# Dilated attention: queries transposed by head and residue, token order copied by GpSimd, and inverse roots by Ln and Exp with one Newton step

## The chip, the cores and the metric

One Trainium2 chip; the kernel runs on one of its cores. The core has engines that work side by side, each through its own queue in order: TensorE (PE in the profile, with its weight loads as PEld), VectorE (DVE), ScalarE (ACT), GpSimd (POOL) and SyncE (SP), which here issues most of the DMA transfers. The metric is the device time in microseconds.

## The reference

One decoder layer over 2048 tokens of width 1024, with 8 attention heads of 64:

```python
h = rms_norm(x, g_mix)
u, gb, gc, q, k, v = split(h @ w_in)
y_conv = gb * short_conv(gc * u, conv_w)
q = rms_norm(q per head, g_q) * HEAD_DIM ** -0.5
k = rms_norm(k per head, g_k)
y_attn = dilated_mixture(q, k, v)
x = x + concat(rms_norm(y_conv), rms_norm(y_attn)) @ w_out
x = x + (silu(h2 @ w_gate) * (h2 @ w_up)) @ w_down      # h2 = rms_norm(x, g_ffn)
```

`rms_norm` is y / sqrt(mean(y^2) + 1e-6) times a gain. `dilated_mixture` evaluates each head three times, with (window, dilation) of (128, 1), (512, 4) and (2048, 16): a query at token t attends to tokens t, t - d, t - 2d, ... within the window. The three outputs of a head are combined with weights in proportion to their softmax denominators. Everything is float32; the kernel gets there with pairs of float16 numbers, a high part and the rest.

## The kernel before, in words

By the trace, the input norm and the convolution's projections take the first 245 us, the first group of q, k and v runs to 300, attention from there to 800, the output projection to 960, the feed-forward network to the end.

Attention works on four head pairs, g = 0 to 3 (`attn_steps`). While pair g is attended, the q, k and v of pair g + 1 are made (`qkv_steps`); beside the last pair runs the rest of the convolution. `attention` draws the two streams together: after each attention step it takes `rate` steps of the other stream, and holds these with `issue_after` behind a mark some `lag` steps back in the attention stream. Within that, the framework's scheduler decides each engine's order (`schedule_with_timeline_sim=True`). Rate and lag are numbers per pair and stay as they are.

`qkv_steps` works in chunks of 512 tokens, 4 for each pair, 16 in all. The 128 rows of a chunk's matmul j are the tokens 4t + j, so a chunk is laid out by residue modulo 4. In a chunk:

- PE makes q, k and v in 4 groups of matmuls into PSUM (L187 to L189); ACT reads q and k out, once as they are (L468) and once squared (L469), and v (L472); DVE takes v's remainder (L473).
- DVE sums the squares (L479) and makes 16 inverse roots for each partition: L480 adds the epsilon, the helper `rsqrt` takes a first guess by integer arithmetic (L45, L46) and does three Newton steps (L48, L49, L50 each), and L482 scales by 2 to the 11th.
- POOL multiplies q and k by the roots (L483) and k by its gain (L486); ACT and POOL split them into high and low parts in `qkhl` (L492 to L495).
- SP issues three DMA transposes (L195): q into `qp`, and the two key tiles `ka` and `kl` (the trace shows `kl` as kb).
- DVE copies `qp` into `qT`, one copy for each head, and in doing so brings the residues back to token order (L504).

`attn_steps` runs, for each head of the pair, the branches b in the order 1, 2, 0, that is dilation 4, 16 and 1. A step is two or four blocks of 128 queries: PE makes scores with the query as the stationary operand and the keys as the moving one (L606, L607, high and low key part), DVE masks them and finds the minimum (L612), ACT takes Exp (L617). Then the weights have to be transposed: most steps do it by ACT's cast (L627), DVE's remainder (L628) and a DMA transpose from `eh` to `et` (L195), the others on PE (L622, L623, L624). PE multiplies with v (L635) and ACT reads the result out (L638). At a head's end `combine` (L542 to L556) joins the three branches, on POOL for every head but the last; DVE makes its weights and ACT their Exp (L546).

In branch 0 the query is a contiguous slice of `qT`, in branch 1 a slice with a stride of 4 elements, in branch 2 one with a stride of 16. The keys lie by residue: contiguous in branch 1, with a stride of 4 in branch 2.

Of the kernel before, what the change touches and what calls it, by code (L numbers as in the profile page):

```python
# [2 lines left out]

# [5 lines left out]
F32 = mybir.dt.float32  # L9
F16 = mybir.dt.float16  # L10
I32 = mybir.dt.int32
AF = mybir.ActivationFunctionType
# [17 lines left out]
class Builder:  # L30
# [167 lines left out]
    def run(self):  # L198
        tc, nc, A = self.tc, self.nc, self.A
        with ExitStack() as ctx:  # L200
# [20 lines left out]
            with ExitStack() as c1:  # L221
                e = c1.enter_context
                self.psmm = e(tc.tile_pool(name="psmm", bufs=3, space=PSUM))
                self.qk = e(tc.tile_pool(name="qk", bufs=4))
# [45 lines left out]
    def conv_steps(self, j, W, before=None, scratch=None):  # L270
# [12 lines left out]
        for c in range(S // NC):  # L283
# [17 lines left out]
            w1 = own[:, 0:2] if own is not None else self.qk.tile([P, 2, NC], F32, name="qT")  # L301
# [26 lines left out]
            nc.scalar.activation(s2, y, AF.Square)  # L328
# [36 lines left out]
    def in_and_conv(self):  # L365
        tc, nc, A = self.tc, self.nc, self.A
        w_in, w_out = A["w_in"][0], A["w_out"][0]
        with ExitStack() as c:
# [23 lines left out]
            def norm(i, n):  # L392
                tags = 6 * ("nx_x",) + ("qT", "qT") + 8 * ("nx_x",)
                self.norm(i, [(self.qk if tg != "nx_x" else xp).tile([P, D], F32, name=tg) for tg in tags[i:i + n]],
# [48 lines left out]
    def qkv_steps(self, g, st):  # L443
# [8 lines left out]
        qT = [self.qk.tile([P, S], F16, name="qT") for _ in range(2)]  # L452

        ka, kl = (self.qk.tile([P, 4, 2, 512], F16, name=nm, bufs=2) for nm in ("ka", "kb"))
        dv = self.d_v[g]
        for i in range(0, NT, 4):
# [22 lines left out]
            nc.vector.tensor_reduce(ss, n, axis=AX.X, op=ALU.add)  # L479
            nc.vector.tensor_scalar(ss, ss, 1.0 / HD, EPS, op0=ALU.mult, op1=ALU.add)  # L480
            r = self.rsqrt(self.at, ss, 16, "qkr")
            nc.vector.tensor_scalar_mul(r, r, 2.0 ** 11)  # L482
# [15 lines left out]
            qp = self.at.tile([P, 2, 4, P], F16, name="qp", bufs=2)  # L498
            for n_, dst in enumerate((qp, ka[:, i // 4].rearrange("p h (j t) -> p h j t", j=4),
                                      kl[:, i // 4].rearrange("p h (j t) -> p h j t", j=4))):  # L500
                self.transpose(dst.rearrange("p h j t -> p (h j) t"),
                               hl[:, 2 * n_:2 * n_ + 2].rearrange("p h j x d -> p (h j x d)"))
            for h in range(2):
                nc.vector.tensor_copy(qT[h][:, i * P:(i + 4) * P].rearrange("p (t j) -> p t j", j=4),  # L504
                                      qp[:, h].rearrange("p j t -> p t j"))
# [3 lines left out]
    def attn_steps(self, g, st):  # L509
# [18 lines left out]
        for h, b in [(h, b) for h in range(2) for b in (1, 2, 0)]:  # L528
            qT = st["qT"][h]
            ka, kl = (st[x][:, :, h] for x in ("ka", "kl"))  # L530
            load_v(h, b)
# [31 lines left out]
            def query(u):  # L563

                if b == 0:
                    return qT[:, u * P:(u + 1) * P]
                if b == 1:
                    return qT[:, u // 4 * 512 + u % 4:(u // 4 + 1) * 512:4]
                return qT[:, u::16]
# [651 lines left out]
```

## Time and profile before

| | |
|---|---|
| runs | 2189.73, 2185.88, 2181.43 us |
| median | 2185.88 us |
| the profiled execution's own time (the span of its trace) | 2189.4 us |
| PE busy over the span | 2068.8 us (94%) |
| DVE | 1457.8 us (67%) |
| ACT | 1025.1 us (47%) |
| POOL | 625.8 us (29%) |
| mean granted PE clock | 0.984 |

The profiled execution has no other time than its span; it lies 3.5 us above the median of the runs. Shares over the whole span hide the stages: half of it is the feed-forward network, in which PE hardly ever waits. The rows to read are those of the stretches from 245 to 800 us. A row of waits names the engine and line that waited, the engine, tile and line that ended the wait, and then the total in us, how often, and the longest one. A row of groups gives the operation with its output and input and its count, then busy us and mean ns of one, then idle time just ahead on the same engine with what ended it.

### The profile page before, as it was taken

The page shows a single profiled execution, that of the slowest core. Times are in us where ns is not written, and L with a number is a line of the kernel's source. Part 1 is how long each engine was busy: PE and PEld are TensorE (multiplying, and loading weights), DVE is VectorE, ACT ScalarE, POOL GpSimd, SP SyncE. Part 2 cuts the span into 40 slices and gives each one's busy share as a digit, 9 for nine tenths or more (in the row PEclk, how much of TensorE's full clock was granted, in tenths as well). Part 3 has the DMA queues.
Part 4 walks back from the last instruction along what each step waited for, and adds up shares of the span by engine and source line. Part 5 has one row for each costly group of instructions (what it writes and reads, how often), then busy time and mean ns, then how long its engine had stood idle before and what let it go on. Part 6 is the DMA issues. An engine that isn't in the chain of part 4 may idle for free. (4 is left out here: it accounts for less than half of the span.)

```text
span 2189.4 us, 32832 instructions
## 1 busy us (share of the span) xinstructions
PE 2068.8 (94%) x11864; PEld 1077.2 (49%) x11864; DVE 1457.8 (67%) x3380; ACT 1025.1 (47%) x2134; POOL 625.8 (29%) x515
## 2 busy tenths in 40 slices
PE   4899999989899889999999999999999999999999
PEld 2344567767666544443444444444444444444444
DVE  5687446778776687795767676756676666545554
ACT  6443346776766656563433333333333334444341
POOL 0000133343443212120232111211121145555463
PEclk9999999999999989999999999999999999999999
DMA  9767458899989996799332233223322663251342
GB/s 245 169 201 243 115 119 153 186 178 178 183 168 202 208 214 216 242 276 263 124 109 87 97 106 101 89 95 101 106 87 97 235 241 105 77 180 54 119 142 96
DMA packets 555492, 339.64 MB, mean 155 GB/s; under 512 B 354624, under 2 KB 508224, under 8 KB 552896
## 3 DMA queue, kind: packets, MB, share of 16 engines
q1 hardware_dynamic: 537648, 314.38, 55.9%
q10 hardware_dynamic: 17680, 23.16, 3.0%
q8 instruction: 93, 1.52, 0.3%
q14 instruction: 71, 0.58, 0.1%
HBM read 161.24 MB, written 107.54 MB: 123 GB/s over the span
## 5 line engine op out<-in xcount | busy, mean ns | idle before, releaser
L1001 PEld LDWEIGHTS <-w 128*128 128x128 f16 x3696 | 362.3, 98 | 454.9 <-issue 20.2
L1001 PE MATMUL ps<-b,w 128*128 128x512 f16 x2112 | 466.5, 382 | 14.0 <-DVE s L1007 6.1
L1132 PE MATMUL ps<-b,w 128*128 128x512 f16 x1848 | 399.8, 379 | 4.0 <-DVE s L1153 2.2
L1001 PE MATMUL ps<-hb,w 128*128 128x512 f16 x1584 | 347.1, 379 | 0.0
L1132 PEld LDWEIGHTS <-w 128*128 128x128 f16 x1848 | 180.8, 98 | 222.9 <-issue 5.4
L187 PE MATMUL mm<-wq,b 128*128 128x384 f16 x512 | 171.8, 335 | 7.1 <-DVE vs L473 7.1
L894 POOL TENSOR_TENSOR t<-wq 128x512 f32<-128x512 f32 (+1 forms) x46 | 59.5, 1294 | 411.4 <-issue 239.0
L1007 DVE TENSOR_TENSOR s<-ps,s 128x512 f32<-128x512 f32 x220 | 150.0, 683 | 34.4 <-PE ps L1001 33.9
L189 PE MATMUL mm<-wq,b 128*128 128x384 f16 x512 | 171.7, 335 | 0.0
L188 PE MATMUL mm<-wq,b 128*128 128x384 f16 x512 | 171.5, 335 | 0.0
L1139 POOL TENSOR_TENSOR x<-x,s 128x512 f32<-128x512 f32 x72 | 103.4, 1436 | 172.6 <-DVE s L1153 134.2
L1140 DVE SCALAR_TENSOR_TENSOR x<-ps,a_u,x 128x512 f32<-128x512 f32 x96 | 71.8, 749 | 100.9 <-PE ps L1132 74.3
L617 ACT ACTIVATE s<-s,u 128x256 f32<-128x256 f32 (+1 forms) x224 | 97.9, 452 | 69.4 <-DVE u L612 50.2
L612 DVE CUSTOM_DVE_ANT_0 s<-s,mask,nkap 128x256 f32<-128x256 f32 (+1 forms) x224 | 104.6, 483 | 19.5 <-PE s L607 13.9
L188 PEld LDWEIGHTS <-b 128*128 128x128 f16 x768 | 84.5, 110 | 67.1 <-issue 18.2
L187 PEld LDWEIGHTS <-b 128*128 128x128 f16 x768 | 84.4, 110 | 61.5 <-ACT b L775 6.4
L911 ACT CAST w<-t 128x512 f16<-128x512 f32 x88 | 53.7, 616 | 127.4 <-PE ps L1001 61.9
L189 PEld LDWEIGHTS <-b 128*128 128x128 f16 x768 | 84.2, 110 | 57.2 <-issue 5.2
L187 PE MATMUL cvx<-b,wq 128*128 128x512 f16 (+1 forms) x200 | 77.0, 388 | 32.1 <-ACT kb L264 24.8
L635 PE MATMUL av<-v,et 128*128 128x65 f16 x1800 | 77.7, 195 | 28.1 <-DMA et<-eh 18.7
L606 PE MATMUL s<-ka,qT 128*128 128x128 f16 (+1 forms) x408 | 91.8, 272 | 10.3 <-DVE eh L628 9.2
L1120 DVE TENSOR_TENSOR w<-t,w 128x512 f16<-128x512 f32 (+1 forms) x96 | 75.3, 801 | 34.2 <-ACT w L1119 33.9
(297 smaller groups left out, 3773.4 us busy)
## 6 DMA issues: line engine op xcount, KB each, us to landing
d_a<-a ACTq DMA_DIRECT2D x88, 256.0 KB, 2.0
d_wd<-w SPq DMA_DIRECT2D x77, 256.0 KB, 2.1
wq<-d_a SPq DMA_DIRECT2D x64, 256.0 KB, 4.2
b<-d_wd SPq DMA_DIRECT2D x14, 1024.0 KB, 6.3
wraw<-in_w_in_dram SPq DMA_DIRECT2D x24, 512.0 KB, 7.2
d_h<-hl SPq DMA_DIRECT2D x24, 512.0 KB, 3.2
wq<-in_w_gate_dram SPq DMA_DIRECT2D x22, 512.0 KB, 5.3
wq<-in_w_up_dram SPq DMA_DIRECT2D x22, 512.0 KB, 5.2
```

The source lines that it names most:

```text
L187: self.pe = mm(ps, lhsT=lh(k), rhs=rh(k), start=k == ks[0], stop=False)
L188: mm(ps, lhsT=lh(k), rhs=rl(k), start=False, stop=False)
L189: mm(ps, lhsT=ll(k), rhs=rh(k), start=False, stop=k == ks[-1])
L606: nc.tensor.matmul(o, lhsT=query(u), rhs=hi[x], start=True, stop=False)
L612: nc.vector.tensor_tensor_reduce(sm[:, at[u]], sp[:, at[u]], mask[:, P - P * has_prev(u):256], accum_out=Ub[:, u, HD + 1:HD + 2], op0=ALU.add,
L617: nc.scalar.activation(sm[:, at[u]], sm[:, at[u]], AF.Exp, scale=-1.0, bias=Ub[:, u, HD + 1:HD + 2])
L635: self.pe_av = nc.tensor.matmul(av[:, u - u0], lhsT=p_, rhs=v_, start=n_ == 0, stop=n_ == len(ops) - 1)
L1001: nc.tensor.matmul(ps[self.BANK[n]], lhsT=w[:, x, k], rhs=b[:, y, k], start=first and k == 0 and q == 0, stop=k == 3 and q == 2, skip_grou ...
L1007: nc.vector.tensor_tensor(t, x, y, op=ALU.add)
L1120: nc.vector.tensor_tensor(L[n][:, 1, 0:n_f], src[n], L[n][:, 0, 0:n_f], op=ALU.subtract)
L1132: nc.tensor.matmul(ps[self.BANK[n]], lhsT=L[n][:, x, f], rhs=B[n][:, f, y], start=first and f == 0 and q == 0, stop=f == n_f - 1 and q == ...
L1139: nc.gpsimd.tensor_tensor(o, o, s_, op=ALU.add)
```

## The change

*The query.* `qT` becomes one tile for both heads, laid out as head, residue j, chunk n, position t. The DMA transpose writes straight into it, so `qp` and DVE's 32 copies are gone. At the start of each head (b == 1) GpSimd copies that head's queries into token order, into a tile `qn` with one buffer, in 4 copies of 128x512. Branch 0 reads `qn`, contiguous as before. Branch 1 now reads a contiguous slice of `qT`, branch 2 one with a stride of 4.

*The inverse roots.* ACT takes Ln of the mean square plus epsilon and Exp of minus half of that plus 11 ln 2, which is the root already scaled by 2 to the 11th; DVE does one Newton step on it. A table that holds both functions is loaded behind the last Square of the convolution, where before the table for Exp was loaded ahead of the first L617; the number of table loads is the same, 5.

*Buffers.* The pool `qk` loses two of its four default buffers, and what shared the tag `qT` (a tile of the convolution, tiles of the norm and of the output projection) takes tiles of twice the size from it.

```diff
--- before.py
+++ after.py
@@ -1,5 +1,6 @@
 from contextlib import ExitStack, nullcontext
 from itertools import chain, islice
+import math
 
 import concourse.bass as bass
 import concourse.tile as tile
@@ -221,7 +222,7 @@
             with ExitStack() as c1:
                 e = c1.enter_context
                 self.psmm = e(tc.tile_pool(name="psmm", bufs=3, space=PSUM))
-                self.qk = e(tc.tile_pool(name="qk", bufs=4))
+                self.qk = e(tc.tile_pool(name="qk", bufs=2))
                 self.mixer(c1)
 
                 self.fs = ctx.enter_context(tc.tile_pool(name="fs", bufs=1, side="right"))
@@ -298,7 +299,7 @@
                 return ps, u
             gc, u = yield from gemm(2)
             own = scratch if c == 0 else None
-            w1 = own[:, 0:2] if own is not None else self.qk.tile([P, 2, NC], F32, name="qT")
+            w1 = own[:, 0:2] if own is not None else pair(c, "qT").rearrange("p (a b) -> p a b", a=2)
             gcs, a = w1[:, 0], w1[:, 1]
             nc.scalar.activation(gcs, gc, AF.Copy, scale=u)
             yield True
@@ -325,7 +326,7 @@
             acc = self.sq[:, c] if j < 3 else s2
             if j == 0:
                 s2 = acc
-            nc.scalar.activation(s2, y, AF.Square)
+            self.sqr = nc.scalar.activation(s2, y, AF.Square)
             if 0 < j < 3:
                 nc.gpsimd.tensor_tensor(acc, acc, s2, op=ALU.add)
                 s2 = acc
@@ -390,8 +391,8 @@
                 W[m] = self.weights([cols(0)[m]], ux, dst=(t0[:, 0, :, cs], t0[:, 1, :, cs]), raw=raw0[:, m])
 
             def norm(i, n):
-                tags = 6 * ("nx_x",) + ("qT", "qT") + 8 * ("nx_x",)
-                self.norm(i, [(self.qk if tg != "nx_x" else xp).tile([P, D], F32, name=tg) for tg in tags[i:i + n]],
+                two = self.qk.tile([P, 2, D], F32, name="qT") if i <= 6 < i + n else None
+                self.norm(i, [two[:, k - 6] if k in (6, 7) else xp.tile([P, D], F32, name="nx_x") for k in range(i, i + n)],
                           [t[:, j] for tg in ("ka", "kb")[i % 4 // 2:(i % 4 + n) // 2]
                            for t in (self.qk.tile([P, 2, 2, D], F16, name=tg, bufs=2),) for j in range(2)])
             spills = []
@@ -449,8 +450,7 @@
         u = self.uq[:, g:g + 1]
         st["u"] = u
         yield
-        qT = [self.qk.tile([P, S], F16, name="qT") for _ in range(2)]
-
+        qT = self.qk.tile([P, 2, 4, 4, P], F16, name="qT")
         ka, kl = (self.qk.tile([P, 4, 2, 512], F16, name=nm, bufs=2) for nm in ("ka", "kb"))
         dv = self.d_v[g]
         for i in range(0, NT, 4):
@@ -477,9 +477,14 @@
             ff = f.rearrange("p a b d -> p (a b) d")
             ss = self.at.tile([P, 16], F32, name="qk_ss")
             nc.vector.tensor_reduce(ss, n, axis=AX.X, op=ALU.add)
+            r = self.at.tile([P, 16], F32, name="qkr_y")
+            t = self.at.tile([P, 16], F32, name="qkr_t")
+            nc.scalar.activation(t, ss, AF.Ln, scale=1.0 / HD, bias=self.lnb[:, 0:1])
+            nc.scalar.activation(r, t, AF.Exp, scale=-0.5, bias=self.lnb[:, 1:2])
             nc.vector.tensor_scalar(ss, ss, 1.0 / HD, EPS, op0=ALU.mult, op1=ALU.add)
-            r = self.rsqrt(self.at, ss, 16, "qkr")
-            nc.vector.tensor_scalar_mul(r, r, 2.0 ** 11)
+            nc.vector.scalar_tensor_tensor(t, r, -0.5 * 2.0 ** -22, r, op0=ALU.mult, op1=ALU.mult)
+            nc.vector.tensor_tensor(t, t, ss, op=ALU.mult)
+            nc.vector.scalar_tensor_tensor(r, t, 1.5, r, op0=ALU.add, op1=ALU.mult)
             nc.gpsimd.tensor_tensor(n, ff, r.unsqueeze(2).broadcast_to([P, 16, HD]), op=ALU.mult)
             n4 = n.rearrange("p (a b) d -> p a b d", a=4)
             nk = n4[:, :, 2:4]
@@ -495,14 +500,10 @@
                 nc.gpsimd.tensor_tensor(hl[:, 4 + h, :, 0], k, hl[:, 2 + h, :, 0], op=ALU.subtract)
 
 
-            qp = self.at.tile([P, 2, 4, P], F16, name="qp", bufs=2)
-            for n_, dst in enumerate((qp, ka[:, i // 4].rearrange("p h (j t) -> p h j t", j=4),
-                                      kl[:, i // 4].rearrange("p h (j t) -> p h j t", j=4))):
-                self.transpose(dst.rearrange("p h j t -> p (h j) t"),
-                               hl[:, 2 * n_:2 * n_ + 2].rearrange("p h j x d -> p (h j x d)"))
-            for h in range(2):
-                nc.vector.tensor_copy(qT[h][:, i * P:(i + 4) * P].rearrange("p (t j) -> p t j", j=4),
-                                      qp[:, h].rearrange("p j t -> p t j"))
+            for n_, dst in enumerate((qT.rearrange("p h j n t -> p (h j) n t")[:, :, i // 4],
+                                      ka[:, i // 4].rearrange("p h (j t) -> p (h j) t", j=4),
+                                      kl[:, i // 4].rearrange("p h (j t) -> p (h j) t", j=4))):
+                self.transpose(dst, hl[:, 2 * n_:2 * n_ + 2].rearrange("p h j x d -> p (h j x d)"))
             yield
         st.update(qT=qT, ka=ka, kl=kl)
 
@@ -526,8 +527,13 @@
                 for r in range(4):
                     nc.sync.dma_start(t[32 * r:32 * r + 32], dv.rearrange("(n p r) c -> r p n c", n=NT, r=4)[r])
         for h, b in [(h, b) for h in range(2) for b in (1, 2, 0)]:
-            qT = st["qT"][h]
+            qT = st["qT"][:, h]
             ka, kl = (st[x][:, :, h] for x in ("ka", "kl"))
+            if b == 1:
+                qn = self.at.tile([P, S], F16, name="qn", bufs=1)
+                for n in range(4):
+                    nc.gpsimd.tensor_copy(qn[:, n * 512:(n + 1) * 512].rearrange("p (t j) -> p t j", j=4),
+                                          qT[:, :, n].rearrange("p j t -> p t j"))
             load_v(h, b)
 
 
@@ -563,10 +569,10 @@
             def query(u):
 
                 if b == 0:
-                    return qT[:, u * P:(u + 1) * P]
+                    return qn[:, u * P:(u + 1) * P]
                 if b == 1:
-                    return qT[:, u // 4 * 512 + u % 4:(u // 4 + 1) * 512:4]
-                return qT[:, u::16]
+                    return qT[:, u % 4, u // 4]
+                return qT[:, u % 4].rearrange("p n t -> p (n t)")[:, u // 4::4]
 
             def keys(tl, u, prev):
 
@@ -695,6 +701,11 @@
         nc.vector.tensor_scalar_mul(self.kap, u, HD ** -0.5 * 2.0 ** -22)
         nc.vector.tensor_scalar_mul(self.nkap, self.kap, -1.0)
 
+        with self.tc.issue_after(self.sqr.ins):
+            nc.scalar.preload_act_table_set("natural_log_exp_and_others")
+        self.lnb = self.at.tile([P, 2], F32, name="lnb")
+        nc.vector.memset(self.lnb[:, 0:1], EPS)
+        nc.vector.memset(self.lnb[:, 1:2], 11 * math.log(2.0))
         self.qkhl = self.at.tile([P, 6, 4, 2, HD], F16, name="qkhl")
         nc.gpsimd.memset(self.qkhl[:, 4:6, :, 1], 0.0)
         self.y7 = self.rows.tile([P, NT, HD], F32, name="y7")
@@ -768,7 +779,7 @@
             ya = tk[:, 0].rearrange("p a (b c) -> p (a b) c", c=2 * P).rearrange("p k (j t) -> p k j t", j=2)
         else:
             ya = self.op.tile([P, 4, 2, P], F32, name="ya")
-        xk = self.qk.tile([P, 2, D], F32, name="kb", bufs=2) if p % 3 == 1 else None
+        xk = self.qk.tile([P, 2, D], F32, name="kb" if p % 3 == 1 else "qT")
         for j in range(2):
             nc.sync.dma_start(ya[:, :, j], self.d_ya[:, :, (p + 8 * j) * P:(p + 8 * j + 1) * P])
         for k in range(4):
@@ -778,7 +789,7 @@
         self.x1[p] = []
         for j in range(2):
             i = p + 8 * j
-            x1 = self.qk.tile([P, D], F32, name="qT") if xk is None else xk[:, j]
+            x1 = xk[:, j]
             nc.sync.dma_start(x1, self.A["x"][0][i * P:(i + 1) * P])
             t = tk[:, 1, j] if p < 2 else self.op.tile([P, 512], F32, name="xt", bufs=2)
```

Line numbers after the change are up by 1 until L480 or so, and by 6 in the attention steps: L612 becomes L618, L617 L623, L627 L633, L628 L634, L638 L644; POOL's L483, L486, L494, L495 become L488, L491, L499, L500, and its L550 to L556 become L556 to L562.

First, DVE around one chunk's inverse roots, during pair 0's attention. ISA is the mask with the minimum (s is a tile of scores), qk_ss the sums of squares, qkr_i, qkr_y and qkr_t the root's tiles. Before:

```order
L480 TENSOR_SCALAR qk_ss<-qk_ss 128x16
L612 ISA s,u<-s,mask,nkap 128x256
L612 ISA u 128x1
L45 TENSOR_SCALAR qkr_i<-qk_ss 128x16
L612 ISA s,u<-s,mask,nkap 128x256
L612 ISA u 128x1
L46 TENSOR_SCALAR qkr_y<-qkr_i 128x16
L48 SCALAR_TENSOR_TENSOR qkr_t<-qkr_y 128x16
L49 TENSOR_TENSOR qkr_t<-qkr_t,qk_ss 128x16
L628 TENSOR_TENSOR eh<-s,eh 128x512
L50 SCALAR_TENSOR_TENSOR qkr_y<-qkr_t,qkr_y 128x16
L553 RECIPROCAL bm<-u 128x16
```

And after the change:

```order
L479 TENSOR_REDUCE qk_ss<-qkn 128x16
L473 SCALAR_TENSOR_TENSOR vs_2120<-mm,vs_2120 128x2x64
L634 TENSOR_TENSOR eh<-s,eh 128x512
L618 ISA s,u<-s,mask,nkap 128x256
L618 ISA u 128x1
L484 TENSOR_SCALAR qk_ss<-qk_ss 128x16
L634 TENSOR_TENSOR eh<-s,eh 128x512
L485 SCALAR_TENSOR_TENSOR qkr_t<-qkr_y 128x16
L618 ISA s,u<-s,mask,nkap 128x256
L618 ISA u 128x1
L486 TENSOR_TENSOR qkr_t<-qkr_t,qk_ss 128x16
L487 SCALAR_TENSOR_TENSOR qkr_y<-qkr_t,qkr_y 128x16
```

Before, the rows shown end in the first Newton step, and seven more rows of the root come behind them (two more steps of L48 to L50, the last rows between masks again, and L482), twelve behind L480 in all. After, three rows behind L484 (which is L480) end the root. The two copies of q for each chunk (L504) have no rows any more.

Second, ACT at the same chunk, after the change (before it there is nothing of the root on ACT):

```order
L633 CAST eh<-s 128x512
L623 ACTIVATE s<-s,u 128x256 x2
L482 ACTIVATE qkr_t<-qk_ss,lnb 128x16
L633 CAST eh<-s 128x512
L483 ACTIVATE qkr_y<-qkr_t,lnb 128x16
L644 COPY u<-av 128x4x65
L623 ACTIVATE s<-s,u 128x256
L468 ACTIVATE qkf<-mm,uq 128x256
```

Ln (L482) stands between the Exp and the cast of score tiles, and Exp of the root (L483) behind that cast. Ln needs DVE's L479, and DVE's L485 needs this Exp.

Third, POOL between a chunk of pair 1 and the combine of a head of pair 0. Before:

```order
L495 TENSOR_TENSOR qkhl<-qkn,qkhl 128x4x64 x2
L550 TENSOR_TENSOR r_3072<-r_3072,cw 128x16x65
L550 TENSOR_TENSOR r_3336<-r_3336,cw 128x16x65
L551 TENSOR_TENSOR r_3072<-r_3072,r_3336 128x16x65
L550 TENSOR_TENSOR u<-u,cw 128x16x65
L552 TENSOR_TENSOR u<-u,r_3072 128x16x65
L556 TENSOR_TENSOR u<-u,bm 128x16x64
L483 TENSOR_TENSOR qkn<-qkf,qkr_y 128x1024
```

And after:

```order
L500 TENSOR_TENSOR qkhl<-qkn,qkhl 128x4x64 x2
L535 COPY qn<-qT 128x512 x4
L556 TENSOR_TENSOR r_3028<-r_3028,cw 128x16x65
L556 TENSOR_TENSOR r_3281<-r_3281,cw 128x16x65
L557 TENSOR_TENSOR r_3028<-r_3028,r_3281 128x16x65
L556 TENSOR_TENSOR u<-u,cw 128x16x65
L488 TENSOR_TENSOR qkn<-qkf,qkr_y 128x1024
L558 TENSOR_TENSOR u<-u,r_3028 128x16x65
```

The four copies into token order stand between the last remainder of a chunk (L500) and the combine (L556), and the next chunk's multiplication by the roots (L488) has moved ahead, into the middle of the combine.

## Prediction

> **What bounds the kernel now.** I read the windows first, one stretch for each stage, since an edit inside attention can only be priced in the stretches where attention runs. The columns are the stretch, its length, then busy time and instruction count of each engine, the granted clock, the share of the DMA engines and their rate:
>
> ```profile
> core 0: us, PE busy (x) PEld busy (x) DVE busy (x) ACT busy (x) POOL busy (x), PEclk, DMA share, GB/s
> 300.00:660.00 360.00, 327.26 (x3167) 250.82 (x3165) 264.83 (x959) 245.99 (x664) 133.07 (x105) 0.96 0.91 175
> 660.00:800.00 140.00, 123.79 (x1149) 79.44 (x1148) 100.68 (x385) 84.12 (x214) 32.24 (x21) 0.94 1.01 219
> 960.00:1790.00 830.00, 815.97 (x3757) 368.09 (x3756) 565.21 (x1032) 319.32 (x567) 180.82 (x145) 0.99 0.42 129
> ```
>
> PE carries the kernel, and the stretch that this change touches is 300 to 660, where three head pairs run with the next pair's q, k and v between them. PE is idle there for 360.0 − 327.3 = 32.7 us. DVE is the busiest of the others (264.8 of 360, 74%), ACT has 68%, POOL 37%, and the DMA engines 0.91. In 660 to 800 the last pair runs without any q and k work. The feed-forward stretch behind it belongs to PE and isn't touched. So no more than 32.7 us of waits, plus whatever PE's own work gets shorter, can be won.
>
> Then PE's waits in that stretch (total us, times, longest):
>
> ```profile
> PE s L606 <- DVE eh L628: 8.9, 6, 2.6
> PE av L635 <- DMA et<-eh: 7.2, 10, 2.0
> PE mm L187 <- DVE vs L473: 6.9, 5, 2.2
> PE av L635 <- DMA v<-d_v: 4.6, 1, 4.6
> PE av L635 <- ACT u L638: 1.8, 1, 1.8
> PE av L635 <- ACT qkn L469: 1.3, 1, 1.3
> PE s L606 <- DVE u L612: 1.1, 2, 0.9
> PE pt L622 <- ACT sm L617: 0.5, 1, 0.5
> PE av L635 <- DVE et L624: 0.3, 1, 0.3
> ```
>
> These add up to 32.6 us, all of PE's idle time. DVE ends 8.9 + 6.9 + 1.1 + 0.3 = 17.2 us of it: PE waits for a PSUM tile that DVE hasn't read out. The et transposes on the DMA queue end 7.2 us, ACT 3.6 us.
>
> **What DVE loses.** The groups of 245 to 800 on DVE (count, then busy us and mean ns, then idle time just ahead and its releaser):
>
> ```profile
> L504 DVE COPY qT<-qp 128x512 f16<-128x512 f16 x32 | 29.9, 976 | 19.3 <-DMA qp<-qkhl 19.2
> L479 DVE TENSOR_REDUCE qk_ss<-qkn 128x16 f32<-128x1024 f32 x16 | 19.5, 1218 | 12.3 <-ACT qkn L469 12.2
> L50 DVE SCALAR_TENSOR_TENSOR qkr_y<-qkr_t,qkr_y 128x16 f32<-128x16 f32 x48 | 10.6, 222 | 1.1
> L48 DVE SCALAR_TENSOR_TENSOR qkr_t<-qkr_y 128x16 f32<-128x16 f32 x48 | 9.4, 197 | 1.0
> L49 DVE TENSOR_TENSOR qkr_t<-qkr_t,qk_ss 128x16 f32<-128x16 f32 x48 | 8.3, 172 | 1.0
> L45 DVE TENSOR_SCALAR qkr_i<-qk_ss 128x16 int32<-128x16 int32 x16 | 5.8, 362 | 0.1
> L482 DVE TENSOR_SCALAR qkr_y<-qkr_y 128x16 f32<-128x16 f32 x16 | 4.7, 297 | 0.4
> L46 DVE TENSOR_SCALAR qkr_y<-qkr_i 128x16 int32<-128x16 int32 x16 | 4.7, 297 | 0.8
> ```
>
> All 32 copies of L504 go (29.9 us), the seed and the final scaling (L45, L46, L482: 15.2 us), and two of three Newton steps (two thirds of 10.6 + 9.4 + 8.3, 18.9 us). That is 64.0 us of DVE time, and with it the 19.2 us in which DVE, an in-order queue, stood still ahead of L504 until the transpose of q had landed. The DMA issues of 300 to 800 (count, median us to landing) show how much of it lies there:
>
> ```profile
> et<-eh SPq DMA_TRANSPOSE x112, 4.2
> qp<-qkhl SPq DMA_TRANSPOSE x14, 3.3
> ```
>
> 14 of the 16 chunks come after 300, so about 56 us leave 300 to 660: DVE falls from 264.8 to about 209 of 360, 58%.
>
> What PE gets of it can't be read off directly. Both large DVE-ended waits are queueing: L628 and L473 are short, but stand behind other DVE work. A queue's wait goes roughly with busy over idle share: 0.74/0.26 = 2.8 now, 0.58/0.42 = 1.4 then, a half less; the blocking ahead of L504 goes too. I estimate that 65% of the 17.2 us goes: **−11.2 us** (bounds: 0, if other engines are late at the same places, and 17.2). The second late thing is the et transpose, which starts when L628 on DVE has written eh. SP waits for that:
>
> ```profile
> SPq L195 <- DVE eh L628: 45.3, 23, 6.4
> SPq L195 <- POOL qkhl L495: 9.9, 4, 4.4
> ```
>
> If L628 comes earlier, the transposes are issued earlier, but they keep their own 4.2 us. I take a third of the 7.2 us: **−2.4 us** (0 to 7.2).
>
> **The query's stride on PE.** Branch 1 read its query with a stride of 4 elements and now reads it contiguously; branch 2 goes from a stride of 16 to 4. The keys, the moving operand, stay as they are, with a stride of 4 in branch 2. First two score matmuls of branch 1, then some of branch 2 with the weight loads beside them (start, duration):
>
> ```profile
> 285.33 0.22 PE L606 MATMUL s<-ka,qT 128*128 128x128 f16 x1
> 285.38 0.22 PE L607 MATMUL s<-kb,qT 128*128 128x128 f16 x1
> ...
> 342.49 0.28 PE L606 MATMUL s<-ka,qT 128*128 128x128 f16 x1
> 342.60 0.30 PE L607 MATMUL s<-kb,qT 128*128 128x128 f16 x1
> 342.71 0.30 PE L606 MATMUL s<-ka,qT 128*128 128x128 f16 x1
> ...
> 342.33 0.14 PEld L606 LDWEIGHTS <-qT 128*128 128x128 f16 x1
> 342.50 0.14 PEld L607 LDWEIGHTS <-qT 128*128 128x128 f16 x1
> ...
> 456.36 0.30 PE L607 MATMUL s<-kb,qT 128*128 128x128 f16 x1
> 456.48 0.34 PE L187 MATMUL mm<-wq,b 128*128 128x384 f16 x1
> ```
>
> Branch 1 starts a matmul every 0.05 to 0.06 us, branch 2 every 0.12. So stride 4 in the weights costs nothing, and branch 1 gains nothing. In branch 2 both operands are strided. The matmul at 342.49 had its weights loaded from 342.33 to 342.47, under the matmul before it, and the next one still starts 0.11 us later; and the last branch-2 matmul, at 456.36, holds up a matmul with another weight tile for 0.12 us. Both point to the moving keys, which the change leaves alone. Branch 2 has 2 × 16 score matmuls in each of 8 heads, 256. If the weights set the pace, 256 × 0.064 = 16.4 us would go; if the keys do, almost nothing. By those two rows I take **−2 us**.
>
> [...]
>
> **What is added to ACT.** 16 chunks × 2 activations of 128x16. The nearest row is a small Exp:
>
> ```profile
> L546 ACT ACTIVATE cw<-cw 128x48 f32<-128x48 f32 (+1 forms) x11 | 2.7, 241 | 8.5 <-DVE cw L545 8.4
> ```
>
> 32 × 0.241 = 7.7 us of ACT, 14/16 of it in the stretch: 246 goes to 253, 70%. The table load only moves. Each chunk now also crosses from DVE to ACT (Ln needs L479's sum) and back (the Newton step needs Exp's result). ACT works in order, so a Ln whose sum is late holds the Exp of scores (L617) behind it, and with it the mask and cast for PE. I raise ACT's 3.6 us by a half: **+1.8 us** (0 to 28, the third rival).
>
> **What is added to POOL and SP.** 32 copies of 128x512 f16. The bounds are a memset of that size and a two-operand f32 operation of that size:
>
> ```profile
> L699 POOL MEMSET qkhl<- 128x512 f16 x1 | 0.5, 524 | 0.0
> L486 POOL TENSOR_TENSOR qkn<-qkn,gk 128x512 f32<-128x512 f32 x16 | 20.4, 1278 | 1.2
> L483 POOL TENSOR_TENSOR qkn<-qkf,qkr_y 128x1024 f32<-128x1024 f32 x16 | 30.5, 1903 | 177.1 <-DVE qkr_y L482 175.3 <-ACT s L617 1.7
> ```
>
> The copy reads with a stride, so I take the upper end, 1.25 us: 40 us in all (17 to 41), some 30 of them in 300 to 660, where POOL goes from 133 to about 163 of 360. They hide in POOL's idle time (177 us ahead of L483 alone), and their result isn't wanted until the third branch. What isn't hidden: four in a row (5 us) ahead of a combine and of the next chunk's L483, whose end (L495) SP's transposes wait for. SP's in-order queue has the et transposes behind them. 5 us more on SP's 9.9, a third of it reaching PE: **+1.7 us** (0 to 10). The transposes move the same bytes. If POOL's cover were gone, all 40 us would stand in the q and k chain.
>
> **Sum.** −11.2 − 2.4 − 2.0 + 1.8 + 1.7 = −12.1 us. The profiled span, 2189.4, lies 3.5 above the median of 2185.88; the saving is taken from either, so 2177.3 for a like profile, and **2174 us** for the median.
>
> **The rivals.** About 11 us (0.5%) is what a measurement of this kernel can tell from no change.
>
> *Another wait takes over: 2183 us.* L628 itself waits: the view of 300 to 660 has it idle behind ACT's cast,
>
> ```profile
> L628 DVE TENSOR_TENSOR eh<-s,eh 128x512 f16<-128x512 f32 (+1 forms) x80 | 54.0, 677 | 20.7 <-ACT eh L627 20.4
> ```
>
> and the DMA share is 0.91 to 1.01. Then ACT or the transposes are late where DVE was, and only about half of the 6.9 us for L473 goes, −3 us. Against it: DVE is the busiest engine beside PE.
>
> *The weights set branch 2's pace: 2160 us.* −12.1 − (16.4 − 2.0) = −26.5. For it: the weight load at a stride of 16 lasts 0.14 us, and the only slow branch is the only one with it. Against: the rows at 342.49 and 456.36.
>
> *ACT's queue is stalled by the crossings: 2198 us.* Place: Ln at the head of ACT's queue, twice 16 crossings. Price: ACT's present waits for DVE,
>
> ```profile
> ACT s L617 <- DVE u L612: 40.3, 27, 5.7
> ```
>
> are 1.5 us each. 32 × 1.5 + 7.7 = 56 us of ACT; with half of it reaching PE, +28 against −15.6 of gains, +12. It decides from about 0.9 us a crossing on. For it: L479 lasts 1.2 us and stands behind other work on DVE. Against: the instructions ahead in ACT's queue are often late themselves, and DVE has become shorter.
>
> **Chances.** The forecast gets 0.46: its terms are sized by rows, except for the 65%. Its own range, 2165 to 2183, has the bound of 2175 inside it, and I put 0.32 of the 0.46 below that bound and 0.14 above. Another wait gets 0.24, the weights 0.14, ACT's queue 0.16. Faster: 0.32 + 0.14 = 0.46; same: 0.14 + 0.24 = 0.38; slower: 0.16. Since cases of both signs are in it, the range that should hold 8 in 10 goes from 2152, below the weights' 2160 by the 6 us that DVE's term could still gain, plus 2 for et, to 2200, just past ACT's case.
>
> **What would show it.** DVE's busy time in 300 to 660 near 209 us, and L606's and L473's waits on DVE at a third; the et waits on DMA near 5 us. Branch 2's matmuls still 0.12 us apart: keys; 0.06: weights. POOL's copies near 1.25 us. ACT's Ln with an idle time ahead of it well under 0.9 us each. I'm wrong if PE's idle time in that stretch stays near 33 us, or if ACT's idle time ahead of Ln goes beyond 30 us.

## The result and the profile after

The changed kernel takes 2169.53 us (median of 4 runs, 2166.6 to 2174.52) against 2186.85 us before (4 runs, three of which stood ahead of the prediction): a ratio of 0.9926, 95% interval 0.9908 to 0.9944, or 17.3 us less. The forecast was 2174, with 2152 to 2200 as its range. The two profiles lie further apart than the medians, 2189.4 and 2165.8 us, or 23.6, since the profiled execution of before was the slowest of its four and that of after lies below its median; so the differences between the two profiles below are some 6 us too large in all.

The windows were cut at the first score matmul and the last product with v, which lie at 285.3 and 803.5 us before and at 285.0 and 776.4 after. Windows of the profile before (columns as above: stretch, length, busy time of PE, PEld, DVE, ACT, POOL, PE clock, DMA share, GB/s):

```profile
285.30:803.50 518.20, 469.25 (x4436) 342.48 (x4434) 375.14 (x1377) 338.20 (x897) 171.96 (x131) 0.96 0.91 182
803.50:2189.00 1385.50, 1357.16 (x6247) 612.13 (x6245) 896.32 (x1556) 564.75 (x1000) 427.77 (x339) 0.99 0.45 138
```

The same two stretches of the profile after:

```profile
285.00:776.40 491.40, 457.83 (x4441) 335.17 (x4440) 330.50 (x1212) 340.96 (x921) 202.49 (x162) 0.98 0.95 192
776.40:2165.00 1388.60, 1360.48 (x6243) 612.79 (x6239) 899.17 (x1564) 565.16 (x1000) 427.86 (x339) 0.99 0.45 138
```

All of the gain lies in attention: 518.2 − 491.4 = 26.8 us; behind it 3.5 us are lost (2189.4 − 803.5 against 2165.8 − 776.4). In attention PE's idle time falls from 48.9 to 33.6 us (−15.4), and its busy time by 11.4 us for the same matmuls, at a granted clock of 0.98 in place of 0.96. Over the whole span the clock differs by 0.002 only (0.984 and 0.986). DVE loses 45 us, POOL gains 31.

PE's waits in attention, after the change (total us, times, longest):

```profile
PE av L641 <- DMA et<-eh: 22.1, 20, 4.2
PE av L641 <- ACT u L644: 6.5, 5, 2.3
PE s L612 <- DVE eh L634: 2.3, 2, 1.7
PE mm L188 <- ACT b L786: 1.2, 1, 1.2
PE av L641 <- DVE et L630: 1.1, 1, 1.1
```

And those of before that answer to them, over its attention:

```profile
PE av L635 <- DMA et<-eh: 18.7, 19, 3.0
PE s L606 <- DVE eh L628: 9.2, 7, 2.6
...
PE av L635 <- DVE et L624: 1.5, 4, 0.6
```

With L473's 6.9 and L612's 1.1, DVE ended 18.7 us of PE's waits before and 3.4 us now, 15.3 less. The one wait for v (4.6 us) is gone too. The waits for et grew by 3.4 us, and those for ACT's read-out of av (L644) by 4.7.

The work of the new root and of the copies, groups of 245 to 777 after the change. On DVE the first two of four rows are shown (L486 and L487 are 4.6 and 2.7 us more), then ACT and POOL:

```profile
L484 DVE TENSOR_SCALAR qk_ss<-qk_ss 128x16 f32<-128x16 f32 x16 | 4.6, 288 | 0.7 <-ACT qkr_t L482 0.7
L485 DVE SCALAR_TENSOR_TENSOR qkr_t<-qkr_y 128x16 f32<-128x16 f32 x16 | 5.4, 337 | 1.1 <-ACT qkr_y L483 1.1
L482 ACT ACTIVATE qkr_t<-qk_ss,lnb 128x16 f32<-128x16 f32 x16 | 5.2, 324 | 6.8 <-DVE qk_ss L479 6.7
L483 ACT ACTIVATE qkr_y<-qkr_t,lnb 128x16 f32<-128x16 f32 x16 | 5.2, 324 | 0.3
L535 POOL COPY qn<-qT 128x512 f16<-128x512 f16 x32 | 34.0, 1097 | 64.4 <-PE s L613 46.2 <-DMA qT<-qkhl 18.3
```

The crossings cost ACT 10.4 us of work and 7.1 us of standing still, over all 16 chunks.

One thing the waits don't say is how early a chunk's q and k are ready. One chunk before (the seventh; the last row of the root on DVE, and the product on POOL that waits for it):

```profile
386.16 1.22 DVE L479 TENSOR_REDUCE qk_ss<-qkn 128x16 f32<-128x1024 f32 x1
395.68 0.17 DVE L482 TENSOR_SCALAR qkr_y<-qkr_y 128x16 f32<-128x16 f32 x1
396.00 1.90 POOL L483 TENSOR_TENSOR qkn<-qkf,qkr_y 128x1024 f32<-128x1024 f32 x1 [1.68 <-ACT s L617]
```

The same chunk after:

```profile
374.45 1.22 DVE L479 TENSOR_REDUCE qk_ss<-qkn 128x16 f32<-128x1024 f32 x1 [0.25 <-ACT qkn L469]
379.70 0.18 DVE L487 SCALAR_TENSOR_TENSOR qkr_y<-qkr_t,qkr_y 128x16 f32<-128x16 f32 x1
379.95 1.90 POOL L488 TENSOR_TENSOR qkn<-qkf,qkr_y 128x1024 f32<-128x1024 f32 x1 [0.89 <-DVE qkr_y L487]
```

From the end of the sum of squares to the start of the product 8.6 us before, 4.3 after. Averaged over all 16 chunks, from the starts and ends of these rows, it is 7.4 and 3.4 us. I call this the root's delay. The split behind it, from the end of that product to the end of POOL's last remainder (L495, then L500), takes 4.6 us before and 5.7 after, since combines and copies stand in between.

### The profile page after: what moved, and what is told of

The parts are those of the page before. It is cut to its first block, busy times and chain, and to the rows that moved or that the text cites. A ratio compares the mean times of both kernels' runs of the same rounds, so it can differ in the third digit from the quotient of the medians.

```text
span 2165.8 us, 32715 instructions
## 1 busy us (share of the span) xinstructions
PE 2062.4 (95%) x11864; PEld 1071.6 (49%) x11864; DVE 1412.4 (65%) x3206; ACT 1031.5 (48%) x2166; POOL 657.8 (30%) x547
## 5 line engine op out<-in xcount | busy, mean ns | idle before, releaser
L188 PE MATMUL mm<-wq,b 128*128 128x384 f16 x512 | 167.7, 327 | 0.0
L189 PE MATMUL mm<-wq,b 128*128 128x384 f16 x512 | 167.5, 327 | 0.0
L190 PE MATMUL mm<-wq,b 128*128 128x384 f16 x512 | 167.4, 327 | 0.0
L618 DVE CUSTOM_DVE_ANT_0 s<-s,mask,nkap 128x256 f32<-128x256 f32 (+1 forms) x224 | 104.4, 483 | 41.4 <-PE s L613 37.1
L623 ACT ACTIVATE s<-s,u 128x256 f32<-128x256 f32 (+1 forms) x224 | 100.0, 457 | 37.4 <-DVE u L618 31.6
L641 PE MATMUL av<-v,et 128*128 128x65 f16 x1800 | 77.5, 195 | 29.9 <-DMA et<-eh 22.1
L634 DVE TENSOR_TENSOR eh<-s,eh 128x512 f16<-128x512 f32 (+1 forms) x112 | 75.6, 678 | 35.4 <-ACT eh L633 35.1
L1121 ACT ACTIVATE wq<-wq,asf 128x512 f32<-128x512 f32 x88 | 56.6, 710 | 86.6 <-DMA wq<-d_a 86.6
```

What stands on the lines that cost most here:

```text
L188: self.pe = mm(ps, lhsT=lh(k), rhs=rh(k), start=k == ks[0], stop=False)
L189: mm(ps, lhsT=lh(k), rhs=rl(k), start=False, stop=False)
L190: mm(ps, lhsT=ll(k), rhs=rh(k), start=False, stop=k == ks[-1])
L618: nc.vector.tensor_tensor_reduce(sm[:, at[u]], sp[:, at[u]], mask[:, P - P * has_prev(u):256], accum_out=Ub[:, u, HD + 1:HD + 2], op0=ALU.add,
L623: nc.scalar.activation(sm[:, at[u]], sm[:, at[u]], AF.Exp, scale=-1.0, bias=Ub[:, u, HD + 1:HD + 2])
L634: nc.vector.tensor_tensor(eh[:, w:2 * w], sm[:, 0:w], eh[:, 0:w], op=ALU.subtract)
```

## The experiments

My theory was that PE waits for DVE and that the gain goes by the DVE time removed, whichever half of the change removes it. The first rival: only the standing still ahead of L504 counts. The second came up on the way: it is the root's delay that counts, not the load. A summary first, all with the kernel before on the same chip; delay and split are means over 16 chunks, attention is from the first score matmul to the last product with v. Attention is read from one profiled execution of each kernel. That of before took 2189.4 us where the medians of before beside the later runs are 2181 to 2182, so its 518.2 is some us too high against the rows below it.

| kernel | ratio to before (95%) | root's delay, split, us | attention, us |
|---|---|---|---|
| before | 1 | 7.4, 4.6 | 518.2 |
| whole change | 0.9926 (0.9908 to 0.9944) | 3.4, 5.7 | 491.4 |
| whole change, lags longer | 0.9955 (0.9943 to 0.9967) | 3.4, 5.5 | 497.7 |
| roots only | 0.9945 (0.9926 to 0.9965) | 3.6, 5.3 | 498.4 |
| query only | 1.0085 (1.0067 to 1.0103) | 6.8, 6.8 | 523.7 |
| query only, lags longer | 1.0053 (1.0040 to 1.0067) | 6.9, 6.8 | 520.2 |
| query only, copies on DVE | 1.0015 (1.0003 to 1.0027) | 7.2, 5.1 | 515.9 |
| whole change, copies on DVE | 0.9951 (0.9932 to 0.9969) | 3.6, 5.5 | 498.5 |
| whole change, product made three times | 1.0102 (1.0088 to 1.0116) | 3.0, 12.1 | 525.5 |
| whole change, more work on DVE | 1.0053 (1.0041 to 1.0065) | 3.5, 7.3 | 520.5 |
| whole change, loose work on DVE | 1.0020 (1.0008 to 1.0031) | 3.5, 5.9 | 497.6 |
| whole change, more work on GpSimd | 0.9943 (0.9926 to 0.9960) | 3.8, 6.7 | 500.1 |
| whole change, no Newton step | 0.9939 (0.9920 to 0.9959) | 1.5, 6.0 | 498.9 |
| whole change, other keys in branch 2 | 0.9892 (0.9871 to 0.9914) | 3.3, 5.8 | 480.9 |

### The two halves

The roots alone: the kernel before with the new roots (Ln, Exp, the Newton step and the earlier table load), and nothing of the query.

```diff
-            r = self.rsqrt(self.at, ss, 16, "qkr")
-            nc.vector.tensor_scalar_mul(r, r, 2.0 ** 11)
+            nc.scalar.activation(t, ss, AF.Ln, scale=1.0 / HD, bias=self.lnb[:, 0:1])
+            nc.scalar.activation(r, t, AF.Exp, scale=-0.5, bias=self.lnb[:, 1:2])
...
+            nc.vector.scalar_tensor_tensor(r, t, 1.5, r, op0=ALU.add, op1=ALU.mult)
```

> The kernel before with the new inverse roots only; the query keeps its copies on DVE. Theory DVE time: the whole change won 17 us by taking 64 us of work and 19 us of standing still from DVE; the roots are 34 of these 83 us, so about -7 us (0.997), and PE's waits ended by DVE in attention fall from 18.7 to about 12 us. Rival blocking: what counts is DVE standing still ahead of the copies of q until the transpose lands; that stays, so 0 to -2 us. Rival ACT: the crossings cost, so 0 or slower here, with PE's waits on ACT up.

Measured: 0.9945, 12 us less, 70% of the whole gain from 34 of the 83 us. Rival blocking allowed 2 us at most and is out as the main cause, since DVE still stands still ahead of the copies of q here (13.9 us). PE's waits on DVE in attention are almost gone:

```profile
PE av L641 <- DMA et<-eh: 25.8, 18, 4.3
PE av L641 <- ACT u L644: 5.9, 5, 3.2
PE av L641 <- DVE et L630: 1.3, 2, 1.1
PE s L612 <- DVE eh L634: 0.7, 2, 0.4
PE pt L628 <- DVE et L630: 0.3, 1, 0.3
```

2.3 us in all, where 12 were expected. So these waits don't go by the time removed.

The query alone: the whole change with the old roots.

```diff
-            nc.scalar.activation(t, ss, AF.Ln, scale=1.0 / HD, bias=self.lnb[:, 0:1])
...
+            r = self.rsqrt(self.at, ss, 16, "qkr")
+            nc.vector.tensor_scalar_mul(r, r, 2.0 ** 11)
```

> The whole change but with the old inverse roots on DVE. Theory DVE time: 49 of the 83 us are gone, about -10 us (0.9955). Rival blocking: -15 us (0.993), nearly the whole gain. If both halves together won more than their sum, the two act on the same waits.

Measured: 1.0085, 18 us slower than before, against −10 expected, although DVE has less to do and no longer stands still for q. PE's waits on DVE are 15.6 us, nearly those of before:

```profile
PE av L636 <- DMA et<-eh: 26.9, 22, 3.8
PE s L607 <- DVE eh L629: 12.9, 7, 3.0
```

The halves alone sum to +6 us; together they are −17. My theory fell here.

### Is it GpSimd, and is it the order?

The whole change with the copies on DVE:

```diff
-                    nc.gpsimd.tensor_copy(qn[:, n * 512:(n + 1) * 512].rearrange("p (t j) -> p t j", j=4),
+                    nc.vector.tensor_copy(qn[:, n * 512:(n + 1) * 512].rearrange("p (t j) -> p t j", j=4),
```

> The whole change, but the 32 copies into token order run on DVE in place of GpSimd. They stand at a head's start, not behind a transpose. Theory DVE time: some 30 us of DVE work are back, the standing still is not: 17 x 53/83 = -11 us (0.995). Rival blocking: -16 us, as the whole change. Rival GpSimd: the copies on GpSimd delay the q and k chain, so this one is faster than the whole change.

Measured: 0.9951, −11 us as by DVE time; about 5 us behind the whole change by the ratios, with intervals that overlap. GpSimd's copies are no loss here.

The same edit in the query alone, so with the old roots:

> The query part alone (old inverse roots), with its 32 copies on DVE in place of GpSimd. If GpSimd's copies made the query part alone slower (+18 and, with longer lags, +12 us), this goes back to 0 or to -5 us (0.9975 to 1.0). If it is the new layout or the order, it stays at +10 us or more (1.0045).

Measured: 1.0015, +3 us. With the old roots the copies on GpSimd cost about 15 us, then, against the same copies on DVE (8 us in the order with longer lags, below); with the new roots they cost nothing. The new layout by itself is no gain.

One step more in each lag, which changes the order and no work:

```diff
-            rate, lag = (4.52, 3.49, 3.2, 2.1)[g], (12, 12, 13, 8)[g]
+            rate, lag = (4.52, 3.49, 3.2, 2.1)[g], (13, 13, 14, 9)[g]
```

> The whole change with each lag one step longer (13, 13, 14, 9): the same work in a slightly different order. It shows how far the order alone moves the time. If every part of the change acts by its size alone, within 3 us of the whole change (0.991 to 0.994). If the order weighs as much as the parts, 10 us or more away from it, either way.

> The query part alone, which was 18 us slower than before, with each lag one step longer. If that loss belongs to the query part by its nature (copies on GpSimd that hold up q and k while the old root is late), it stays at +14 us or more (1.0065). If it belongs to one unlucky order, it shrinks to below +8 us or turns into a gain.

Measured: 0.9955 and 1.0053. The whole change loses 6 us by it and the query alone gains 7. So the order alone moves these kernels by 6 to 7 us, which bounds what can be read from smaller differences in the table; the query's loss is about 18 us in one order and 12 in the other.

### Delay or load?

GpSimd makes the product of q and k with the roots three times, with the same result:

```diff
-            nc.gpsimd.tensor_tensor(n, ff, r.unsqueeze(2).broadcast_to([P, 16, HD]), op=ALU.mult)
+            for _ in range(3):
+                nc.gpsimd.tensor_tensor(n, ff, r.unsqueeze(2).broadcast_to([P, 16, HD]), op=ALU.mult)
```

> The whole change, but GpSimd multiplies q and k by the roots three times over (the same product each time), so that each chunk's q and k come 3.8 us later; DVE's work stays cut. Measured before: from the end of the sum of squares to the start of that product 7.35 us a chunk on average before, 3.4 with the whole change, 3.6 with the roots alone. Theory latency: the gain comes from this shorter chain, so it goes back to about -3 us (0.9985). Theory DVE time: GpSimd has idle time there and DVE is as short as in the whole change, so -14 us or more (0.9935).

Measured: 1.0102, 22 us slower than before, 38 us slower than the whole change, for 61 us of GpSimd (32 products of 1.914 us). Attention starts 4 us later (288.9 us) and takes 34 us longer. In the table its delay is that to the first product, and its split holds the other two. Its groups of 245 to 815 show that GpSimd was far from full:

```profile
L489 POOL TENSOR_TENSOR qkn<-qkf,qkr_y 128x1024 f32<-128x1024 f32 x48 | 91.8, 1914 | 117.9 <-DVE qkr_y L487 88.3 <-ACT s L624 23.2 <-ACT sm L624 4.4
```

It stands idle for 117.9 us ahead of these products alone. DVE's busy time in attention is that of the whole change (330.7 and 330.5 us), so the added products don't act by holding up DVE's own operations. And yet PE waits for DVE for 14.5 us again, and for 7.7 us, which the whole change does not have, for the transposes of q and k:

```profile
PE s L613 <- DVE eh L635: 7.5, 8, 2.0
PE s L613 <- DMA qT<-qkhl: 5.2, 2, 4.2
PE mm L188 <- DVE vs L473: 4.8, 4, 2.2
...
PE s L614 <- DMA kb<-qkhl: 2.5, 2, 2.3
```

The counterpart puts work on GpSimd behind the chunk's last remainder, outside the chain, reading that remainder so that it can't run ahead:

```diff
+            for _ in range(4):
+                nc.gpsimd.tensor_copy(self.zc.rearrange("p (d j b) -> p j d b", j=4, b=2),
+                                      hl[:, 5, :, 0].unsqueeze(3).broadcast_to([P, 4, HD, 2]))
```

> The whole change plus 4 copies of 128x512 f16 on GpSimd for each chunk, behind the chunk's last split, whose result they read so that they cannot run ahead: about 4.4 us a chunk, 70 us in all, more than the 61 us put into the chain in the run with the late root, but outside the chain. Theory latency: only the time until q and k stand in their tile counts, so -12 us or more stay (0.9945). Theory GpSimd load: whatever GpSimd gets extra costs as it did there, +15 us or more (1.007).

Measured: 0.9943, still −12 us, so within 4 us of the whole change.

```profile
L502 POOL COPY zc<-qkhl 128x512 f16<-128x512 f16 x64 | 42.3, 661 | 2.5
```

The copies were cheaper than expected (42 us, not 70). Still, 42 us outside the chain cost nothing that can be told apart from an order's 6 us, and 61 us inside cost 38; at the rate of the latter, 42 us would have cost 26. So it is the time until q and k stand in their tile that counts, and not GpSimd's load. PE's waits for DVE are back here as well (12.5 us in attention) while those for et fall to 17.0: what ends a wait last changes from run to run, and one row of waits alone does not tell what a kernel loses.

Work on DVE, behind the root and reading it, on which nothing depends:

```diff
+            nc.vector.tensor_copy(self.zs, r)
+            for _ in range(8):
+                nc.vector.tensor_scalar(self.zs, self.zs, 1.0 / HD, EPS, op0=ALU.mult, op1=ALU.add)
+            for _ in range(3):
+                nc.vector.tensor_copy(self.zc.rearrange("p (a b) -> p a b", a=16),
+                                      self.zs.unsqueeze(2).broadcast_to([P, 16, 32]))
```

> The whole change, with some 4 us of work for each chunk put back on DVE behind the root, reading the root so that it cannot run ahead (one copy, 8 operations of 128x16, 3 copies of 128x512), 60 us in all; nothing depends on it, so the root and the query are as early as in the whole change. Theory DVE time: back to -4 us (0.998). Theory latency: stays at -13 us or more (0.994). The run before it with loose work on DVE did not tell this, because most of that work ran ahead of attention.

Measured: 1.0053, 28 us slower than the whole change, with PE's waits on DVE back at 18.4 us:

```profile
PE s L618 <- DVE eh L640: 15.6, 12, 3.1
...
PE av L647 <- DVE et L636: 1.5, 2, 1.1
...
PE mm L188 <- DVE vs L473: 1.3, 1, 1.3
```

It was a larger dose than planned:

```profile
L488 DVE COPY zs<-qkr_y 128x16 f32<-128x16 f32 x16 | 8.9, 558 | 0.4
L490 DVE TENSOR_SCALAR zs<-zs 128x16 f32<-128x16 f32 x128 | 75.7, 591 | 2.9
L492 DVE CAST zc<-zs 128x512 f16<-128x512 f32 x48 | 28.8, 600 | 1.3
```

113 us, not 60, since the small operations took 591 ns each, against 268 ns in the run with loose work below. The root's delay stays at 3.5 us; the split behind it grew by 1.6. So DVE's load counts too, at about 28/113, a quarter of a microsecond for each (a third, if only the 88 us by which DVE's busy time grew in attention are counted). The split's growth can hardly carry much of it: the run with work on GpSimd has nearly the same delay and split (10.5 us together, against 10.8) and an attention that is 20 us shorter.

An earlier form of this run, with loose work on DVE (9 operations on a constant tile and 2 copies for each chunk), settled nothing:

> The whole change plus work on DVE on which nothing depends: behind each chunk's root 9 operations of 128x16 and 2 strided copies of 128x512 f16, so some 50 to 60 us of DVE time come back, without waiting for any transpose. Theory DVE time: the gain shrinks to about -4 to -6 us, and PE's waits ended by DVE come back to 10 us or more. Rival blocking, or the order of the engines: the gain stays at -15 us or more, with PE's waits on DVE below 5 us.

It came to 1.0020 (1.0008 to 1.0031), but most of the work ran ahead of attention (all 32 copies and 97 of the 144 small operations before 300 us), where the wait it made is plain, and attention only started at 298 us:

```profile
PE mm L188 <- DVE vs L473: 12.3, 3, 11.6
```

Less delay still: the Newton step is left out, so the root is Exp's result as it is.

```diff
-            nc.vector.tensor_scalar(ss, ss, 1.0 / HD, EPS, op0=ALU.mult, op1=ALU.add)
-            nc.vector.scalar_tensor_tensor(t, r, -0.5 * 2.0 ** -22, r, op0=ALU.mult, op1=ALU.mult)
-            nc.vector.tensor_tensor(t, t, ss, op=ALU.mult)
-            nc.vector.scalar_tensor_tensor(r, t, 1.5, r, op0=ALU.add, op1=ALU.mult)
```

> The whole change without the Newton step: the root is Exp's result as it is, so the inverse root is less exact. Takes 4 DVE operations (19 us in all by the whole change's rows) and their time out of the chain, 1 us a chunk or more. Theory of DVE time and latency: 5 to 12 us faster than the whole change (0.987 to 0.990). If both are used up, no more than 2 us.

Measured: 0.9939, no gain over the whole change, with a delay of 1.5 us. From 3.4 us on, less doesn't help. What is late here is et's transposes:

```profile
PE av L637 <- DMA et<-eh: 26.5, 23, 2.5
```

### What sets the pace in branch 2

The whole change shows the first half of the answer: with the query's stride at 4, branch 2's score matmuls still start 0.12 us apart.

```profile
384.79 0.28 PE L612 MATMUL s<-ka,qT 128*128 128x128 f16 x1
384.89 0.30 PE L613 MATMUL s<-kb,qT 128*128 128x128 f16 x1
385.01 0.30 PE L612 MATMUL s<-ka,qT 128*128 128x128 f16 x1
385.13 0.30 PE L613 MATMUL s<-kb,qT 128*128 128x128 f16 x1
```

For the other half, branch 2 reads a contiguous block of keys in place of those with a stride of 4, so it leaves out the dilation and its result is not the reference's:

```diff
-                return [k[:, :, u % 4, u // 4::4]]
+                return [k[:, u // 4:u // 4 + 1, u % 4]]
```

> The whole change, but branch 2 reads other keys: a contiguous block of the same size in place of the one with a stride of 4, so that branch scores against the wrong keys. The whole change has the query at a stride of 4 there and its matmuls still start every 116 ns at the median. If the moving keys set the pace: 56 ns, up to 15 us off PE, and 5 to 15 us faster than the whole change. If it is something else in that branch: 116 ns still and the same time.

Measured: 0.9892, some 7 us below the whole change, with intervals that overlap, and

```profile
382.71 0.22 PE L612 MATMUL s<-ka,qT 128*128 128x128 f16 x1
382.77 0.22 PE L613 MATMUL s<-kb,qT 128*128 128x128 f16 x1
```

0.06 us apart. The moving keys set the pace. It is the stride and not the step over four chunks that these keys also have: branch 0's first blocks read their keys as four runs of 32 contiguous elements and start 0.056 us apart. 256 × 0.06 = 15 us of PE are in the stride, and PE's busy time in attention falls by as much (457.8 to 442.2 us). About half reach the end, by a difference that is hardly larger than what the order alone moves.

## Why the prediction was right, and where it wasn't

Direction, place and rough size held: 2169.5 against 2174, all of it in attention, and the largest term was the right one. PE's idle time in 300 to 660 fell from 32.7 to 18.9 us, so the sign of being wrong did not show. That the total came so close is in part luck: DVE's term was too small by 4 us and two items were not in the sum at all, and against these stands a term of the wrong sign. DVE's busy time in 300 to 660 is 240.7 us, not 209; the stretch now holds 4% more of PE's work (341.1 against 327.3 us), which explains a part of that. Point by point:

- *PE's waits on DVE, −11.2 us.* They fell by 15.3 (18.7 to 3.4). The reason given, a queue that goes by DVE's load, was only half of it. By that reason the copies of q, 49 of the 83 us, should have brought more than the roots; the runs give the roots −12 us and the query alone, with DVE freed of the copies, +12 to +18. This step failed in its division. What it left out is the root's delay: twelve small operations in a chain behind L480, most of them queued between masks and remainders, against Ln, Exp and three operations. The delay went from 7.4 to 3.4 us, and a run that lengthened the same chain by 3.8 us on another engine lost 38 us.
- *The transposes of et, −2.4 us.* Wrong in sign: 18.7 to 22.1 us, and 7.2 to 14.3 in the prediction's own stretch, 300 to 660. With PE no longer held by DVE, the transposes are what is late next. The first rival named this; it took effect after DVE's gain, not in place of it.
- *The query's stride, −2 us.* The start-to-start time of branch 2's 256 matmuls fell from 120 to 117 ns at the median (the 116 of the expectation above also counts branch 0's first blocks), 256 × 0.003 = 0.8 us. That the keys set the pace, as the two rows had it, is shown. The weights' rival is out: with the query at a stride of 4 in place of 16, matmuls on f16 keys at a stride of 4 still start 0.12 us apart, where those on contiguous keys start 0.06 us apart.
- *ACT, +1.8 us.* PE's waits on ACT in attention rose from 6.8 to 7.7 us, that is +0.9, with the same kinds of work counted (L638 with L469, L617 and L775 before, L644 and L786 after). In 300 to 660 alone they fell, from 3.6 to 2.7. Ln stood still for 6.8 us, 0.4 a chunk, and Exp for 0.3, so 0.2 a crossing. The third rival was to decide from 0.9 a crossing on; by its own sum, half of (32 crossings + 7.7 us) against 15.6 us of gains, it breaks even at 0.73. The measured 0.2 is well below either.
- *GpSimd and SP, +1.7 us.* The copies took 1.10 us, not 1.25. SP's waits for GpSimd in 300 to 660 rose from 9.9 to 15.6 us (7.1 for the remainder, 8.5 for the copies), near the 5 us more that were forecast; what of it reached PE no run separates. That GpSimd's idle time hides them is right with the new roots only. With the old ones the same copies made 8 to 15 us of difference, by the order. The prediction had this as a sentence ("If POOL's cover were gone") and not as an interaction of the two halves.
- *Not foreseen.* The single wait for v, 4.6 us, went. And PE's busy time in attention fell by 11.4 us, of which the stride explains 0.8. The runs show that this goes with the length of attention: with the keys as they are, PE is busy for 458 to 463 us in every kernel whose attention takes 491 to 500 us, and for 468 to 471 in every one with 516 to 526. So in the slower kernels about 10 us of PE's busy time come on top of the waits. The granted clock of the stretch doesn't explain it by itself (0.95 with 459 us in the roots alone, 0.95 with 471 in the query alone); why it is so stays open.

What stays open is through which wait the delay reaches PE. In the kernels with a late root the loss shows up in different rows, behind DVE's remainder in one, behind ACT or the transposes of q and k in another. Nor is the sum of delay and split a measure by itself. The run with other keys aside, attention takes 491 to 500 us where the two sum to 10.5 us or less, and 516 to 526 where they sum to 10.8 or more; but the two runs at that border differ in DVE's load, and from 12.0 to 15.1 us of sum attention grows by 7 us only. Of these runs, one lengthened the chain on purpose and one put load on the same engine outside it.

## What to carry to other kernels

Two streams share in-order engines here, and a chain of small operations cost more by the delay it gathered than by its busy time: 34 of the 83 us of DVE time, taken out of such a chain, brought 12 of the 17 us, and 61 us put into it cost 38. Load outside the chain cost where the engine was the busy one: 113 us on DVE cost 28, 42 us on GpSimd nothing that could be told. Price the halves of a change apart and ask what each does to the other's cover: here the two halves alone sum to no gain, and together they win. And before pricing a stride, look at which operand the matmuls wait for; in branch 2 it was the moving one (0.12 us from start to start at a stride of 4, 0.06 contiguous).

## What the runs showed of the hardware

Some of the old root's small operations on DVE and some of the copies of q, whose operands all lie in SBUF, were seen to stretch beside a GpSimd operation until about its end. In the kernel before, 11 of the root's took 0.55 to 2.17 us each, where those with GpSimd idle took 0.17 us on average; the 11 ended within 0.04 us of a GpSimd operation's end, and the 7 long copies 0.45 to 0.47 us after one. DVE and POOL in the seventh chunk:

```profile
387.89 1.76 DVE L480 TENSOR_SCALAR qk_ss<-qk_ss 128x16 f32<-128x16 f32 x1
391.90 0.13 DVE L48 SCALAR_TENSOR_TENSOR qkr_t<-qkr_y 128x16 f32<-128x16 f32 x1
392.86 1.48 DVE L48 SCALAR_TENSOR_TENSOR qkr_t<-qkr_y 128x16 f32<-128x16 f32 x1
...
387.23 2.40 POOL L552 TENSOR_TENSOR u<-u,r 128x1040 f32<-128x1040 f32 x1
392.40 1.92 POOL L556 TENSOR_TENSOR u<-u,bm 128x1024 f32<-128x1024 f32 x1 [2.78 <-DVE qkr_t L49]
```

L48 takes 0.13 us, and 1.48 us when it starts within L556; it ends at 394.34, 0.02 us after L556. L480 ends with L552. Over the whole trace the copies of L504 take 0.60 us where GpSimd is idle (25 of 32) and 2.32 us where it runs for more than half of their time (7); the mean of 976 ns that the prediction used is a mixture of the two. The masks (L612), whose scores come from PSUM, show nothing of it: 487 ns at 128x256 with GpSimd idle, 488 beside it. Nor does the sum of squares (L479), which reads SBUF alone: 1.22 us with GpSimd idle and beside it. Why the one stretches and the other does not, no run shows.

The old root's small operations lost 13 us to this over the 16 chunks, 0.8 of the 7.4 us of delay. It is also why the work put on DVE behind the root, where GpSimd starts its product, cost 591 ns an operation: the 41 small operations without any GpSimd work beside them took 0.17 us, the 82 with it for more than half of their time 0.83 us.
